# First layer's gate vectors: eight of 24 column blocks as whole dot products beside the last feature tiles' keys and values

## The chip, the cores and the metric

The kernel runs on one core of one Trainium2 chip. The metric is the device time of one execution in microseconds. TensorE (PE) multiplies, VectorE (DVE), ScalarE (ACT) and GpSimd (POOL) compute on tiles of 128 partitions, and SyncE (SP) issues all of this kernel's transfers, in order, from one queue. Each engine carries out its own instructions in order and waits where an operand or a buffer is not there yet.

## The reference

A trunk of two layers over 1024 latent tokens (`x`) and 256 context tokens (`ctx`), each 1024 wide. Cut to what matters here:

```python
silu_c, silu_cc = silu(c), silu(c_ctx)                  # two conditioning vectors of 1024
for i in range(2):
    shift, scale, gate = split(silu_c @ w_ada[i] + b_ada[i], 3)         # w_ada[i]: 1024 x 3072
    shift_c, scale_c, gate_c = split(silu_cc @ w_ada[i] + b_ada[i], 3)
    u  = h  * (1 + scale)   + shift
    uc = hc * (1 + scale_c) + shift_c
    y, yc = mixer(u, uc)          # layer 0: windowed attention, 4 key/value heads, rotary; layer 1: 2-D neighbourhood
    h  = layer_norm(sqrt(2) * h  + gate   * y)
    hc = layer_norm(sqrt(2) * hc + gate_c * yc)         # layer 0 only
```

The shift and scale of layer 0 are wanted first of all, since every feature of `u` hangs on them. The gate of layer 0 is wanted only after its attention, and with it the shift and scale of layer 1. These are 24 column blocks of 128 outputs, for two vectors each.

## The kernel before

All products are made in fp32 from a high and a low part of each operand (`hi`, `lo`, `wh`, `wl`, `uAh`, `uAl`): three matmuls stand for one.

**Start.** Features are taken in eight tiles (`kt`). For each, `mod_load` fetches the modulation weights (two tiles `wada` of 512 KB, from a ring of ten buffers) and the feature rows `hraw` (ring of four); `mod_rows` and `mod` make shift and scale on TensorE; `u_make` makes `uAh` and `uAl`; `k_mm` and `v_mm` add the tile's part to the keys (four PSUM banks `kp0_0`, `kp0_1`, `kp1_0`, `kp1_1`, and `kc`) and to the values of the first 512 tokens (`vps`). Value weights (`wv`) lie in buffers of the ring of ten too.

**After the last tile.** `rope_evac` turns the keys: VectorE shuffles a bank into `rb` and multiplies the bank by `cos` into `ra` (both read PSUM), GpSimd multiplies `rb` by `sin`, VectorE adds the two; `k_store` splits the sum into a tile `st` (ScalarE the high, VectorE the low part), which goes to memory (`kdA`). Meanwhile TensorE makes the values of the other tokens (`vproj_pieces`, banks `pv-1_2`, `pv-1_3`, `pv-1_4`) and the first query projection (`qprojA(0)`, banks `pj8_0` to `pj8_2`). The four banks of the keys are the only ones for these, so each waits for an eviction. The weights of a projection are split on the way: `wh` on ScalarE, `wl` on GpSimd; `wh8`/`wl8` hold features 0 to 511 and `wh9`/`wl9` the rest for `qprojA(0)`.

**Attention of layer 0.** Eight segments (`p`), each with 20 softmax blocks and, merged between them, the projections of the next heads. Beside them run the 24 column blocks, written as 48 half dots (`dot_half(h, j)`): a tile `gw` of 128 outputs by 512 inputs is loaded, VectorE reduces its product with `silu_c` (L617), GpSimd multiplies it by `silu_cc` (L618), and ScalarE sums that up (L599, issued with the next half dot by `dot_sum`). The numbers `SEG` say how many go into each segment; `dots_end` adds the halves and the bias.

What sets the order: the code is written in one sequence, and a list scheduler with priorities moves instructions on each engine, within the dependencies. The order on an engine is thus read from the built program, not from the code.

Of the kernel before, what the change touches and what calls it, by code (L numbers as in the profile page):

```python
# [11 lines left out]
F32 = mybir.dt.float32  # L12
F32R = mybir.dt.float32r
BF16 = mybir.dt.bfloat16
AF = mybir.ActivationFunctionType
ALU = mybir.AluOpType
# [3 lines left out]
P = 128  # L20
D = 1024
S = 1024
C = 256
T = S + C
# [13 lines left out]

GATED_LAST = 1 << 20

SEG = (7, 7, 7, 7, 7, 7, 6, 0)


def f32(ap):
# [38 lines left out]
def build(tc, i, out):  # L83
    nc = tc.nc
    mm = nc.tensor.matmul
    dma = nc.sync.dma_start
# [26 lines left out]
    dcol = cp.tile([P, 32, 2], F32, name="dcol")  # L113
# [4 lines left out]
    vdA = dr.tile([T, 4, P], F32, name="vdA")  # L118
# [140 lines left out]
    def v_evac(pl, vd):  # L259
        def evac(pt, b):  # L260
            st = st_tile(pl)
            for t in range(2):
                v = st[:, t].rearrange("p (h l d) -> p h l d", h=4, l=2)
                src = pt[:, t * 256 : (t + 1) * 256].rearrange("p (h d) -> p h d", h=4)
                nc.scalar.activation(v[:, :, 0, :], src, AF.Copy, scale=0.5)
                nc.vector.scalar_tensor_tensor(v[:, :, 1, :], src, 0.5, f32(v[:, :, 0, :]), ALU.mult, ALU.subtract)
            t0 = 2 * b * P
            dma(vd[t0 : t0 + 2 * P].rearrange("(t p) h e -> p t (h e)", p=P), f32(st))

        return evac  # L270
# [13 lines left out]
    def merge(att, fill, lead=0.0):  # L284

        ta = sum(a[0] for a in att) or 1.0
        tf = sum(f[0] for f in fill)
        ia = jf = 0
        ca = cf = 0.0
        while ia < len(att) or jf < len(fill):  # L290
            need = att[ia][2] if ia < len(att) and len(att[ia]) > 2 else 0
            if jf < len(fill) and (ia == len(att) or jf < need or cf - lead <= ca * (tf - lead) / ta):
                cf += fill[jf][0]
                fill[jf][1]()
                jf += 1
            else:
                ca += att[ia][0]
                att[ia][1]()
                ia += 1
# [162 lines left out]
    def rope_evac(store, pl, bufs):  # L462
        def evac(pt, t0, n):
            if t0 >= S:
                store(pt[:, :n], t0, n)
                return
            a = pl.tile([P, 512], F32, tag="ra", bufs=bufs, name="ra")
            b = pl.tile([P, 512], F32, tag="rb", bufs=bufs, name="rb")
            nc.vector.stream_shuffle(b, pt, SWAP)
            nc.vector.tensor_tensor(a, pt, cos[:, t0 : t0 + n], ALU.mult)  # L470
            nc.gpsimd.tensor_tensor(b, b, sin[:, t0 : t0 + n], ALU.mult)
            nc.vector.tensor_tensor(a, a, b, ALU.add)
            store(a, t0, n)

        return evac

    def k_store(nt):
        def store(src, t0, n):
            st = st_tile(pp)
            nc.scalar.copy(st[:, 0, :n], src)  # L480
            nc.vector.tensor_tensor(st[:, 1, :n], src, f32(st[:, 0, :n]), ALU.subtract)
            dma(kdA[:, nt * P : (nt + 1) * P, t0 : t0 + n].rearrange("l p t -> p l t"), f32(st[:, :, :n]))

        return store
# [67 lines left out]
    def v_mm(kt):  # L552
        hi, lo = w.got[VALUES[kt // 2]]
        sl = slice((kt % 2) * 256, (kt % 2 + 1) * 256)
        for t in range(4):
# [3 lines left out]
            mm(pt, lh, lo[:, sl], start=False, stop=False)  # L559
            mm(pt, ll, hi[:, sl], start=False, stop=kt == KT - 1 and t % 2 == 1)  # L560


    upto = (2, 3, 4, 4, 6, 7, 8, 8)
    for kt in range(-1, KT + 1):
        if kt + 1 < KT:
            for n in range(3) if kt < 0 else (kt + 3,) if kt + 3 < KT else ():
                mod_load(n, upto[n])
                if n == 0:
                    w.split(2)
            mod_rows(kt + 1)  # L570
        if kt > 0:
            k_mm(kt - 1)
        if kt + 1 < KT:
            mod(kt + 1)
        if kt < 0:

            warm(vps[:, 0:512], 12)
        if kt > 0:
            v_mm(kt - 1)
        if kt < KT and kt >= 0:  # L580
            u_make(kt)
            w.split(upto[min(kt + 1, 7)])
    dma(ident, i["ident"])
    dma(lnc, i["lnc"])
    dma(cos, i["cos"])
# [4 lines left out]


    dhalf = cp.tile([P, 24, 2], F32, name="dhalf")
    gh, sums = [], []

    def dot_sum():

        if sums:
            t, acc = sums.pop()
            tc.keep_in_program_order(nc.scalar.activation(t, t, AF.Copy, scale=0.5, accum_out=acc))  # L599

    def dot_half(h, j):
        def run():
            dot_sum()
            if j == 0:
                gh.clear()
                for v in range(2):
                    t = px.tile([P, 512], F32, tag=f"gh{v}", bufs=1, name="gh")
                    dma(t, bass.AP(i["cr"].tensor, v * D + h * 512, [[0, P], [1, 512]]))
                    th = px.tile([P, 512], F32, tag="gw", bufs=2, name="gth")
                    nc.scalar.activation(th, t, AF.Tanh, scale=0.5)  # L610
                    nc.vector.scalar_tensor_tensor(t, th, 1.0, t, ALU.add, ALU.mult)
                    gh.append(t)
            acc = dhalf if h else dcol
            t = px.tile([P, 512], F32, tag="gw", bufs=2, name="gw")
            dma(t, i["wadaT"][j, :, h * 512 : (h + 1) * 512])
            o = ap_.tile([P, 512], F32, tag="ra", bufs=1, name="gj")
            nc.vector.tensor_tensor_reduce(o, t, gh[0], 0.5, 0.0, ALU.mult, ALU.add, accum_out=acc[:, j, 0:1])  # L617
            nc.gpsimd.tensor_tensor(t, t, gh[1], ALU.mult)  # L618
            sums.append((t, acc[:, j, 1:2]))

        return (0.0, run, 0)

    def dots_end():
        dot_sum()
        for v in range(2):
            d = dcol[:, 0:24, v]
            nc.vector.tensor_tensor(d, d, dhalf[:, 0:24, v], ALU.add)
            nc.vector.tensor_tensor(d, d, bad[:, 16:40], ALU.add)
            shift, scale = dcol[:, 8:16, v], dcol[:, 16:24, v]
            nc.vector.scalar_tensor_tensor(colA[:, v, :], scale, 1.0, lnc[:, 0, :], ALU.add, ALU.mult)  # L630
            nc.vector.scalar_tensor_tensor(colB[:, v, :], scale, 1.0, lnc[:, 1, :], ALU.add, ALU.mult)
            nc.vector.tensor_tensor(colB[:, v, :], colB[:, v, :], shift, ALU.add)

    dots = [dot_half(h, j) for h in range(2) for j in range(24)]
    evs = []
    for c, (t0, n) in enumerate(CHUNKS):
        for nt in range(2):
            pt = kps[c, nt] if c < 2 else kc[:, nt * C : nt * C + C]
            evs.append((1.0, lambda nt=nt, pt=pt, t0=t0, n=n: rope_evac(k_store(nt), pp, 2)(pt, t0, n)))
    merge(evs, [])  # L640
    for b in range(2):
        v_evac(pp, vdA)(vps[:, b * 512 : (b + 1) * 512], b)
    merge([], vproj_pieces(-1, uA, v_evac(pp, vdA), 2))
    pp_st.close()
    pq, pq_st = pool("attA", "right")

# [692 lines left out]
```

## Time and profile before

| | us |
|---|---|
| median of three runs (lowest, highest) | 1449.84 (1449.49, 1455.52) |
| the profiled execution's own time | 1450.25 |
| its span | 1448.5 |
| TensorE busy in the span | 1393.6 (96%) |
| VectorE, ScalarE, GpSimd busy | 988.8, 733.9, 631.7 |
| granted TensorE clock, mean | 0.994 |

The time of an execution is 1.75 us longer than its span. A row of a timeline reads: start, duration, engine, line, operation, output<-inputs, shapes, count, and in brackets how long the engine stood idle before it and what ended that. A row of a group ends in: busy time, mean ns of one | idle time before, and what ended it. Engines in brackets after "waits" or "<-" are the ones that were waited for.

### The profile page before, as it was taken

The numbers are of one execution on the slowest core, as the hardware profiler recorded it, in microseconds if no ns is written. First come the engines' busy times: TensorE is split into PE (matmuls) and PEld (weight loads), VectorE is DVE, ScalarE is ACT, GpSimd is POOL, SyncE is SP. The second block draws the span as 40 slices with busy tenths as digits, with TensorE's granted clock in tenths as the row PEclk, the third lists the DMA queues.
The fourth block names the chain that finished last, engine by engine and source line by source line (L and its number), as shares of the span: only waits on it lengthen the run. The fifth ranks groups of instructions, "written<-read, shape, count | busy, mean of one in ns | idle before, by whom it ended". The sixth has DMA issues, their size and how long they took to land. (4 is left out here: it accounts for less than half of the span.)

```text
span 1448.5 us, 25148 instructions
## 1 busy us (share of the span) xinstructions
PE 1393.6 (96%) x8815; PEld 1217.2 (84%) x8816; DVE 988.8 (68%) x2216; ACT 733.9 (51%) x1561; POOL 631.7 (44%) x779
## 2 busy tenths in 40 slices
PE   8998999999999999999999999999999999998995
PEld 5887888888888888788888899888988898887775
DVE  4658887878888789566423766555565565667698
ACT  4336776677676778332222545554454444557310
POOL 0326666666666657233301333333233333336664
PEclk9999999999999999999999999999999999999998
DMA  9472114123222124434278565565555564384353
GB/s 369 172 227 85 60 48 131 45 77 101 68 70 62 56 67 131 133 129 136 75 216 230 156 195 152 150 166 146 168 147 152 146 182 140 102 207 151 114 133 93
DMA packets 117229, 195.05 MB, mean 135 GB/s; under 512 B 9328, under 2 KB 57840, under 8 KB 117104
## 3 DMA queue, kind: packets, MB, share of 16 engines
q1 hardware_dynamic: 117104, 193.45, 44.4%
q8 instruction: 70, 1.15, 0.3%
q14 instruction: 55, 0.45, 0.1%
HBM read 141.51 MB, written 51.90 MB: 134 GB/s over the span
## 5 line engine op out<-in xcount | busy, mean ns | idle before, releaser
L329 POOL TENSOR_SCALAR s_B<-s_B,rs_B 128x640 f32<-128x640 f32 (+1 forms) x128 | 101.1, 790 | 298.0 <-DVE rs_B L328 243.9
L208 PE MATMUL pj<-uBh,wh 128*128 128x512 f32 (+1 forms) x448 | 176.0, 393 | 0.0
L209 PE MATMUL pj<-uBl,wh 128*128 128x512 f32 (+1 forms) x448 | 170.3, 380 | 0.0
L210 PE MATMUL pj<-uBh,wl 128*128 128x512 f32 (+1 forms) x448 | 170.1, 380 | 0.0
L324 ACT ACTIVATE s_B<-s_B,m_B 128x640 f32<-128x640 f32 (+1 forms) x128 | 102.9, 804 | 131.2 <-DVE m_B L317 131.1
L324 ACT ACTIVATE s_A<-s_A,m_A 128x641 f32<-128x641 f32 (+2 forms) x160 | 119.5, 747 | 88.7 <-DVE m_A L317 73.7
L164 POOL TENSOR_TENSOR wl<-wr,wh 128x512 fp32r<-128x512 f32 x64 | 87.7, 1370 | 162.1 <-ACT wh L162 139.8
L329 POOL TENSOR_SCALAR s_A<-s_A,rs_A 128x640 f32<-128x640 f32 (+2 forms) x160 | 126.8, 793 | 58.0 <-DVE rs_A L328 55.7
L317 DVE CUSTOM_DVE_ANT_0 s_A<-S_A,msk,nsk 128x640 f32<-128x640 f32 (+2 forms) x160 | 123.6, 774 | 34.1 <-PE S_A L705 17.7
L342 DVE TENSOR_TENSOR pt_B<-T_B,pt_B 128x640 fp32r<-128x640 f32 (+1 forms) x128 | 100.9, 788 | 61.0 <-ACT pt_B L340 60.6
L208 PE MATMUL pj<-uAh,wh 128*128 128x512 f32 (+1 forms) x384 | 140.0, 365 | 0.0
L209 PE MATMUL pj<-uAl,wh 128*128 128x512 f32 (+1 forms) x384 | 137.8, 359 | 0.0
L210 PE MATMUL pj<-uAh,wl 128*128 128x512 f32 (+1 forms) x384 | 137.5, 358 | 0.0
L342 DVE TENSOR_TENSOR ptl_A<-T_A,pth_A 128x640 fp32r<-128x640 f32 (+2 forms) x160 | 114.0, 713 | 15.3 <-PE pvA L733 7.1
L336 PE MATMUL T_A<-ident,s_A 128*128 128x128 f32 x672 | 101.1, 275 | 12.2 <-DVE m_A L317 8.9
L336 PEld LDWEIGHTS T_A<-ident,s_A 128*128 128x128 f32 x672 | 77.2, 140 | 40.2 <-issue 16.7
L340 ACT CAST pt_B<-T_B 128x640 fp32r<-128x640 f32 (+1 forms) x128 | 84.3, 658 | 47.6 <-PE T_B L336 46.6
L317 DVE CUSTOM_DVE_ANT_0 s_B<-S_B,bias 128x640 f32<-128x640 f32 (+1 forms) x128 | 100.4, 784 | 10.5 <-PE S_B L1036 9.7
L340 ACT CAST pth_A<-T_A 128x640 fp32r<-128x640 f32 (+2 forms) x160 | 96.4, 603 | 16.8 <-PE T_A L336 14.1
L210 PEld LDWEIGHTS pj<-uBh,wl 128*128 128x128 f32 x448 | 84.3, 188 | 16.6
L336 PE MATMUL T_B<-ident,s_B 128*128 128x128 f32 x608 | 88.7, 275 | 9.9 <-DVE pt_B L342 5.0
L242 PE MATMUL pv<-wh,uBh 128*128 128x256 f32 x320 | 92.8, 291 | 3.1 <-ACT wh L162 3.1
(219 smaller groups left out, 3883.6 us busy)
## 6 DMA issues: line engine op xcount, KB each, us to landing
kB<-kdB SPq DMA_DIRECT2D x64, 320.0 KB, 5.2
gw<-in_wadaT SPq DMA_DIRECT2D x48, 256.0 KB, 2.8
vdB<-st SPq DMA_DIRECT2D x20, 512.0 KB, 3.2
vB<-vdB SPq DMA_DIRECT2D x16, 640.0 KB, 4.7
wada<-in_wadaC SPq DMA_DIRECT2D x16, 512.0 KB, 9.6
kdB<-st SPq DMA_DIRECT2D x16, 512.0 KB, 3.0
qdB<-st SPq DMA_DIRECT2D x16, 512.0 KB, 3.5
qB<-qdB SPq DMA_DIRECT2D x32, 256.0 KB, 4.7
```

What stands on the lines that cost most here:

```text
L164: e.tensor_tensor(lo, r, f32(hi), ALU.subtract)
L208: mm(pt[:, :n], hi[:, sl], rh, start=kt == 0, stop=False)
L209: mm(pt[:, :n], hi[:, sl], rl, start=False, stop=False)
L210: mm(pt[:, :n], lo[:, sl], rh, start=False, stop=kt == KT - 1)
L242: mm(pt, lh, hi[:, sl], start=kt == 0, stop=False)
L317: nc.vector.tensor_tensor_reduce(outp, sc, in1, scale, init if init is not None else 3e38, ALU.add, ALU.min, accum_out=s.m)
L324: nc.scalar.activation(s.t[:, :n], s.t[:, :n], AF.Exp, bias=s.m, scale=-1.0, accum_out=s.sum)
L329: nc.gpsimd.tensor_scalar(s.t[:, : s.w], s.t[:, : s.w], s.rs, 1.0, ALU.mult, ALU.mult)
L336: nc.tensor.transpose(tp[:, k * P : (k + 1) * P], s.t[:, src * P : (src + 1) * P], ident)
L340: nc.scalar.copy(pt.hi[:, :n, hl, :], tv)
L342: nc.vector.tensor_tensor(pt.lo[:, :n, hl, :], tv, f32(pt.hi[:, :n, hl, :]), ALU.subtract)
```

## The change

Column blocks 0 to 7 (the gate of layer 0; `PRE = 8`) leave attention and are made as whole dot products of 1024 inputs in the early stage. For that, the two vectors are loaded to all partitions (`silb`) and their silu (twice its value) is made there, once `mod_rows` of the later tiles has released buffers of the ring of ten; the weight tiles `gp0` to `gp7` come into the same ring. Each block is then one reduction on VectorE (`dcol[:, j, 0]`), one product in place on GpSimd, and one sum on ScalarE, as the half dots are, but twice as long. `early` puts the start of it beside tiles 5 to 7, and `pre_step` the rest between the evictions of the keys and the pieces of the values. The scratch output of the reduction takes a buffer of `hraw`. In attention 32 half dots (blocks 8 to 23) are left of 48, at most five a segment instead of seven.

```diff
--- before.py
+++ after.py
@@ -38,7 +38,8 @@
 
 GATED_LAST = 1 << 20
 
-SEG = (7, 7, 7, 7, 7, 7, 6, 0)
+PRE = 8
+SEG = (5, 5, 5, 5, 4, 4, 4, 0)
 
 
 def f32(ap):
@@ -559,6 +560,54 @@
             mm(pt, lh, lo[:, sl], start=False, stop=False)
             mm(pt, ll, hi[:, sl], start=False, stop=kt == KT - 1 and t % 2 == 1)
 
+    sums = []
+
+    def dot_sum():
+
+        if sums:
+            t, acc = sums.pop()
+            tc.keep_in_program_order(nc.scalar.activation(t, t, AF.Copy, scale=0.5, accum_out=acc))
+
+
+    dcol_pre, silb = {}, []
+
+    def pre_load(j):
+        dcol_pre[j] = pp.tile([P, D], F32, tag="wada", bufs=10, name=f"gp{j}")
+        dma(dcol_pre[j], i["wadaT"][j])
+
+    def pre_dot(j):
+        t = dcol_pre.pop(j)
+        o = pp.tile([P, T], F32, tag="hraw", bufs=4, name="junk")[:, :D]
+        nc.vector.tensor_tensor_reduce(o, t, silb[0], 0.5, 0.0, ALU.mult, ALU.add, accum_out=dcol[:, j, 0:1])
+        nc.gpsimd.tensor_tensor(t, t, silb[1], ALU.mult)
+        sums.append((t, dcol[:, j, 1:2]))
+
+    def early(kt):
+        if kt == 5:
+            for v in range(2):
+                t = pp.tile([P, D], F32, tag="wada", bufs=10, name=f"silb{v}")
+                dma(t, bass.AP(i["cr"].tensor, v * D, [[0, P], [1, D]]))
+                silb.append(t)
+        if kt == 6:
+            pre_load(0)
+            for t in silb:
+                th = pp.tile([P, T], F32, tag="hraw", bufs=4, name="th")[:, :D]
+                nc.scalar.activation(th, t, AF.Tanh, scale=0.5)
+                nc.vector.scalar_tensor_tensor(t, th, 1.0, t, ALU.add, ALU.mult)
+        if kt == 7:
+            pre_load(1)
+            pre_dot(0)
+        if kt == 8:
+            pre_step(2)
+
+    def pre_step(j):
+
+        dot_sum()
+        if j < PRE:
+            pre_load(j)
+        if j - 1 < PRE:
+            pre_dot(j - 1)
+
 
     upto = (2, 3, 4, 4, 6, 7, 8, 8)
     for kt in range(-1, KT + 1):
@@ -580,6 +629,7 @@
         if kt < KT and kt >= 0:
             u_make(kt)
             w.split(upto[min(kt + 1, 7)])
+        early(kt)
     dma(ident, i["ident"])
     dma(lnc, i["lnc"])
     dma(cos, i["cos"])
@@ -590,18 +640,12 @@
 
 
     dhalf = cp.tile([P, 24, 2], F32, name="dhalf")
-    gh, sums = [], []
-
-    def dot_sum():
-
-        if sums:
-            t, acc = sums.pop()
-            tc.keep_in_program_order(nc.scalar.activation(t, t, AF.Copy, scale=0.5, accum_out=acc))
+    gh = []
 
     def dot_half(h, j):
         def run():
             dot_sum()
-            if j == 0:
+            if j == PRE:
                 gh.clear()
                 for v in range(2):
                     t = px.tile([P, 512], F32, tag=f"gh{v}", bufs=1, name="gh")
@@ -623,24 +667,29 @@
     def dots_end():
         dot_sum()
         for v in range(2):
+            d = dcol[:, PRE:24, v]
+            nc.vector.tensor_tensor(d, d, dhalf[:, PRE:24, v], ALU.add)
             d = dcol[:, 0:24, v]
-            nc.vector.tensor_tensor(d, d, dhalf[:, 0:24, v], ALU.add)
             nc.vector.tensor_tensor(d, d, bad[:, 16:40], ALU.add)
             shift, scale = dcol[:, 8:16, v], dcol[:, 16:24, v]
             nc.vector.scalar_tensor_tensor(colA[:, v, :], scale, 1.0, lnc[:, 0, :], ALU.add, ALU.mult)
             nc.vector.scalar_tensor_tensor(colB[:, v, :], scale, 1.0, lnc[:, 1, :], ALU.add, ALU.mult)
             nc.vector.tensor_tensor(colB[:, v, :], colB[:, v, :], shift, ALU.add)
 
-    dots = [dot_half(h, j) for h in range(2) for j in range(24)]
+    dots = [dot_half(h, j) for h in range(2) for j in range(PRE, 24)]
     evs = []
     for c, (t0, n) in enumerate(CHUNKS):
         for nt in range(2):
             pt = kps[c, nt] if c < 2 else kc[:, nt * C : nt * C + C]
             evs.append((1.0, lambda nt=nt, pt=pt, t0=t0, n=n: rope_evac(k_store(nt), pp, 2)(pt, t0, n)))
+    evs = evs[:2] + [(1.0, lambda: pre_step(3))] + evs[2:4] + [(1.0, lambda: pre_step(4))] + evs[4:]
     merge(evs, [])
     for b in range(2):
         v_evac(pp, vdA)(vps[:, b * 512 : (b + 1) * 512], b)
-    merge([], vproj_pieces(-1, uA, v_evac(pp, vdA), 2))
+    pv = vproj_pieces(-1, uA, v_evac(pp, vdA), 2)
+    for n in range(PRE - 2):
+        pv.insert(1 + 5 * n, (0.0, lambda j=5 + n: pre_step(j)))
+    merge([], pv)
     pp_st.close()
     pq, pq_st = pool("attA", "right")
 
```

What the scheduler makes of it is seen at three places. On VectorE, after the last feature tile (`uAl` are its low parts; `kp0_0` is the first key bank; an ISA with `junk` is a reduction, the next one the read of its accumulator), the rows before are:

```order
L539 TENSOR_TENSOR uAl0_108<-hraw_472,uAh0_105 128x512
L539 TENSOR_TENSOR uAl2_110<-hraw_472,uAh2_107 128x256
L588 TENSOR_SCALAR nsk_142<-nsk_142 128x16
L469 STREAM_SHUFFLE rb_735<-kp0_0_144 128x512
L470 TENSOR_TENSOR ra_734<-kp0_0_144,cos_139 128x512
L469 STREAM_SHUFFLE rb_745<-kp0_1_145 128x512
L472 TENSOR_TENSOR ra_734<-ra_734,rb_735 128x512
L470 TENSOR_TENSOR ra_744<-kp0_1_145,cos_139 128x512
L469 STREAM_SHUFFLE rb_755<-kp1_0_146 128x512
```

and now:

```order
L596 SCALAR_TENSOR_TENSOR silb1_600<-th_666,silb1_600 128x1024
L581 ISA junk_710,dcol_71<-gp0_661,silb0_598 128x1024
L581 ISA dcol_71 128x1
L581 ISA junk_746,dcol_71<-gp1_708,silb0_598 128x1024
L581 ISA dcol_71 128x1
L470 STREAM_SHUFFLE rb_758<-kp0_0_144 128x512
L470 STREAM_SHUFFLE rb_768<-kp0_1_145 128x512
L581 ISA junk_780,dcol_71<-gp2_744,silb0_598 128x1024
L581 ISA dcol_71 128x1
L471 TENSOR_TENSOR ra_757<-kp0_0_144,cos_139 128x512
```

The second scaling of a silu row (the first stands ahead of `uAl0`) and three reductions, two ahead of the shuffles and one behind them, now come before the first product with `cos`, which is the last row. On GpSimd, in the same stretch (`rb` are the keys' sine products), before:

```order
L164 TENSOR_TENSOR wl8_946<-wr8_794,wh8_945 128x512
L471 TENSOR_TENSOR rb_735<-rb_735,sin_140 128x512
L164 TENSOR_TENSOR wl9_956<-wr9_796,wh9_955 128x512
L471 TENSOR_TENSOR rb_745<-rb_745,sin_140 128x512
L164 TENSOR_TENSOR wl10_986<-wr10_983,wh10_985 128x512
L471 TENSOR_TENSOR rb_755<-rb_755,sin_140 128x512
L164 TENSOR_TENSOR wl11_992<-wr11_989,wh11_991 128x512
L471 TENSOR_TENSOR rb_765<-rb_765,sin_140 128x512
L471 TENSOR_TENSOR rb_1025<-rb_1025,sin_140 128x512
```

and now:

```order
L582 TENSOR_TENSOR gp0_661<-gp0_661,silb1_600 128x1024
L582 TENSOR_TENSOR gp1_708<-gp1_708,silb1_600 128x1024
L582 TENSOR_TENSOR gp2_744<-gp2_744,silb1_600 128x1024
L472 TENSOR_TENSOR rb_758<-rb_758,sin_140 128x512
L472 TENSOR_TENSOR rb_768<-rb_768,sin_140 128x512
L472 TENSOR_TENSOR rb_784<-rb_784,sin_140 128x512
L472 TENSOR_TENSOR rb_794<-rb_794,sin_140 128x512
L165 TENSOR_TENSOR wl8_1004<-wr8_829,wh8_1003 128x512
L582 TENSOR_TENSOR gp3_778<-gp3_778,silb1_600 128x1024
L582 TENSOR_TENSOR gp4_804<-gp4_804,silb1_600 128x1024
L165 TENSOR_TENSOR wl9_1014<-wr9_831,wh9_1013 128x512
L582 TENSOR_TENSOR gp5_841<-gp5_841,silb1_600 128x1024
```

Before, GpSimd has the low parts `wl8` and `wl9` first and third in this stretch; now three products of 1024 and four sine products precede `wl8`, and two more products precede `wl9`. On VectorE, at the eviction of the values (`vps`) and of the first query bank `pj8_0`, before:

```order
L481 TENSOR_TENSOR st_774<-kc_148,st_774 128x256
L481 TENSOR_TENSOR st_778<-kc_148,st_778 128x256
L266 SCALAR_TENSOR_TENSOR st_782<-vps_149,st_782 128x4x64 x2
L266 SCALAR_TENSOR_TENSOR st_788<-vps_149,st_788 128x4x64 x2
L266 SCALAR_TENSOR_TENSOR st_847<-pv-1_2_798,st_847 128x4x64 x2
L266 SCALAR_TENSOR_TENSOR st_902<-pv-1_3_853,st_902 128x4x64 x2
L469 STREAM_SHUFFLE rb_1025<-pj8_0_999 128x512
```

and now:

```order
L581 ISA junk_910,dcol_71<-gp6_871,silb0_598 128x1024
L581 ISA dcol_71 128x1
L267 SCALAR_TENSOR_TENSOR st_817<-vps_149,st_817 128x4x64 x2
L581 ISA junk_938,dcol_71<-gp7_908,silb0_598 128x1024
L581 ISA dcol_71 128x1
L267 SCALAR_TENSOR_TENSOR st_823<-vps_149,st_823 128x4x64 x2
L470 STREAM_SHUFFLE rb_1083<-pj8_0_1057 128x512
L471 TENSOR_TENSOR ra_1082<-pj8_0_1057,cos_139 128x512
L267 SCALAR_TENSOR_TENSOR st_894<-pv-1_2_833,st_894 128x4x64
```

Reductions 6 and 7 stand between the value evictions, and `pj8_0` is read ahead of the banks `pv-1_2` and `pv-1_3` instead of behind them. With that goes another allocation of banks: `pj8_1` now takes the bank of `pj8_0`, where before it took that of `pv-1_2`. On SyncE's queue the loads of `silb`, `gp0`, `gp1` and `gp2` stand ahead of `ident`, `cos`, `sin` and the masks; `gp3` and `gp4` ahead of the first query weights; `gp5` to `gp7` between the stores of the keys; and `wr14` and `wr15`, which wait for GpSimd's `wl12` and `wl13`, ahead of the loads of `kA` instead of behind them.

## Prediction

> **What bounds the kernel now.** I read the page first, then the busy time by stretches, then TensorE's timeline through the first layer, and last VectorE and GpSimd where the change puts its work.
>
> ```profile
> span 1448.5 us, 25148 instructions
> PE 1393.6 (96%) x8815; PEld 1217.2 (84%) x8816; DVE 988.8 (68%) x2216; ACT 733.9 (51%) x1561; POOL 631.7 (44%) x779
> 58.00:98.00 40.00, 40.00 (x270) 37.11 (x269) 26.65 (x44) 11.77 (x25) 16.91 (x12) 1.00 0.58 186
> 98.00:165.00 67.00, 61.47 (x394) 53.42 (x393) 53.98 (x131) 44.74 (x103) 43.75 (x62) 1.00 0.35 100
> 165.00:527.00 362.00, 351.07 (x2285) 307.72 (x2283) 296.17 (x720) 251.64 (x573) 234.75 (x341) 1.00 0.23 73
> ```
>
> In the stretch rows the columns after the length are the busy time of TensorE (PE), its weight load, VectorE (DVE), ScalarE (ACT) and GpSimd (POOL). TensorE is the bound. Between 58 and 98 us (last feature tile, values, first projection) it has no gap at all, so any wait put there lengthens the run one for one. From 98 to 527 us, where the 48 half dots lie, it is idle for 5.53 + 10.93 = 16.5 us. That is all that the taking away of dots could ever give back; adding dots to the first stretch can only cost.
>
> How much of the 16.5 us belongs to dots shows in TensorE's and VectorE's rows beside them:
>
> ```profile
> 125.29 0.74 PE L336 MATMUL T_A<-ident,s_A 128*128 128x128 f32 x5 [1.30 <-POOL gw L618]
> 249.21 1.52 DVE L617 CUSTOM_DVE_ANT_0 gj<-gw,gh 128x512 f32<-128x512 f32 x1 [0.46 <-DMA gw<-in_wadaT]
> 251.70 0.74 PE L336 MATMUL T_A<-ident,s_A 128*128 128x128 f32 x5 [1.16 <-DVE m_A L317]
> 374.66 0.74 PE L336 MATMUL T_A<-ident,s_A 128*128 128x128 f32 x5 [1.16 <-DVE m_A L317]
> ```
>
> Three gaps have a dot directly ahead of them, 1.30 + 1.16 + 1.16 = 3.6 us; the rest repeats in every segment where the short context tiles are.
>
> **The change, part by part: what attention gets back.** Sixteen half dots leave the segments (48 become 32). Their busy time is no gain by itself, because TensorE covers it; the gain lies between 0 (the same gaps behind other dots) and the 3.6 us of the three gaps. With a third of the dots gone one gap of three would go by chance; wider spacing helps too. I take 2.0 us. One more gap could open behind a dot at a new place, up to 1.3 us as in the row at 125.29, so the lower end is -1.3. The final additions in dots_end keep their count.
>
> **What the early stage pays.** Eight whole dots are added, and two silu rows. The nearest prices:
>
> ```profile
> L617 DVE CUSTOM_DVE_ANT_0 gj<-gw,gh x48: 671/694/1523, 114.2 to 522.6; 128x512 f32<-128x512 f32 x48
> L618 POOL TENSOR_TENSOR gw<-gw,gh x48: 1262/1290/1306, 115.0 to 523.8; 128x512 f32<-128x512 f32 x48
> L909 DVE SCALAR_TENSOR_TENSOR z<-z,yA 128x1024 f32<-128x1024 f32 x9 | 10.9, 1210 | 0.0
> L1214 POOL TENSOR_TENSOR x<-x,vec 128x1024 f32<-128x1024 f32 x8 | 20.7, 2582 | 9.5 <-DMA x<-zdd 9.5
> L599 ACT ACTIVATE gw<-gw 128x512 f32<-128x512 f32 x48 | 30.2, 629 | 6.0 <-POOL gw L618 5.8
> L915 ACT ACTIVATE z<-z,rsd 128x1024 f32<-128x1024 f32 x10 | 12.4, 1243 | 34.3 <-issue 21.2 <-DVE rsd L914 13.1
> ```
>
> A whole dot is one reduction of 1024 on VectorE (1.25 us with its accumulator read), one product of 1024 on GpSimd (2.58 us) and one sum on ScalarE (1.24 us and a read of 0.19). Eight of them are 10.0 us of VectorE, 20.7 us of GpSimd and 11.4 us of ScalarE. By busy time all three fit into the 40 us stretch (26.65, 16.91 and 11.77 were used). They do not fit by order, for GpSimd and VectorE shut each other out:
>
> ```profile
> 61.95 1.28 POOL L164 TENSOR_TENSOR wl<-wr,wh 128x512 fp32r<-128x512 f32 x1
> 62.02 1.75 DVE L472 TENSOR_TENSOR ra<-ra,rb 128x512 f32<-128x512 f32 x1 [0.16 <-POOL rb L471]
> 63.19 1.76 POOL L471 TENSOR_TENSOR rb<-rb,sin 128x512 f32<-128x512 f32 x1
> 63.70 0.68 DVE L470 TENSOR_TENSOR ra<-kp,cos 128x512 f32<-128x512 f32 x1
> 72.68 0.69 DVE L472 TENSOR_TENSOR ra<-ra,rb 128x512 f32<-128x512 f32 x1
> ```
>
> L472 takes 0.69 us alone and 1.75 beside GpSimd's L164: it starts only when L164 is done, and GpSimd's L471 then waits for it. L470, which reads PSUM, runs beside GpSimd at 0.68. So where both operands are in SBUF the two engines take turns. Now the rows of the present stage that set the deadlines:
>
> ```profile
> 53.99 1.43 ACT L538 CAST uAh<-hraw 128x512 fp32r<-128x512 f32 x3
> 59.45 0.39 PE L550 MATMUL kp<-uAl,wh 128*128 128x512 f32 x1
> 63.88 0.28 PE L242 MATMUL pv-1_2_798<-wv,uAh 128*128 128x256 f32 x1
> 75.40 0.28 PE L242 MATMUL pv-1_4_908<-wv,uAh 128*128 128x256 f32 x1
> 81.16 0.39 PE L208 MATMUL pj<-uAh,wh 128*128 128x512 f32 x1
> 83.89 0.39 PE L208 MATMUL pj<-uAh,wh 128*128 128x512 f32 x1
> 86.61 0.39 PE L208 MATMUL pj<-uAh,wh 128*128 128x512 f32 x1
> 37.73 0.33 SPq L585 DMA_DIRECT2D cos<-in_cos  x1
> 50.39 1.08 PE L509 MATMUL kc<-wada,sil 128*32 128x128 f32 x32
> kA<-kdA SPq DMA_DIRECT2D x16, 320.0 KB, 5.0
> ```
>
> The silu rows: the two tanh (1.24 each) stand between the three casts of the last tile on ScalarE, the two scalings (1.2 each) between the three subtractions on VectorE. The last uAl ends near 58.0 instead of 56.2; TensorE asks for it at 59.45. Covered, cost 0; were silb late, this cover of 1.5 us would go. On SyncE's queue gp2 waits for the last modulation weights (51 us, the row at 50.39), and cos, sin and the masks stand behind it: issued near 52 instead of 37.7, landed near 57. VectorE asks for cos after 65. Cost 0.
>
> Then, instruction by instruction in the new order. (From here on, line numbers are those of the changed code, which are one higher in the evictions: its L471, L473 and L482 on VectorE are L470, L472 and L481 of the rows above.) The second scaling ends at 59.2, reduction 0 at 60.5, reduction 1 at 61.8; product 0 runs 61.8 to 64.4, and the two shuffles beside it; reduction 2 gets its turn at 64.4 to 65.7, and only then comes L471's reading of kp0_0 (66.4 us), on whose bank pv-1_2 waits: a stall of **2.5 us** against 63.88. Without the turn (reduction 2 at 63.2) it would be 1.2. GpSimd goes on with products 1 and 2 to 70.9 and the four sine products to 81.2, since each pair waits for VectorE to hand over a shuffled tile; kp1_0 is read at 78.6, against 75.40 + 2.5 for pv-1_4: **0.7 us**. Then turn by turn: reduction 3 (82.5), wl8 (83.7), L473 (84.3), product 3 (86.9), L482 and reduction 4 (88.8), L482 (89.4), product 4 (92.0), reduction 5 (93.3), wl9 (94.6). TensorE wants wl9 at the third matmul of the row at 83.89, 84.35 + 3.2 = 87.6: **7.0 us**. With no turns GpSimd would need 20.7 us of work and two hand-overs of some 1.5 us from 60.5 on, and wl9 would be there at 84.2: 0. I keep 7.0, since every pair in the rows above takes turns.
>
> No row shows a reduction (L617) holding GpSimd up: L618 never leaves 1262 to 1306 ns, for it always follows its own reduction. The Trainium skill (SBUF — State Buffer, "Who interferes with whom") says that an instruction of VectorE with two SBUF inputs contends with one of GpSimd that reads SBUF, and that whoever issues first has the port pair for its whole length. By that rule the reductions block GpSimd as L472 does, and the figure stays 7.0; were the reductions to block nothing, four times 1.25 us would leave the chain, and the stall would be 2.
>
> Next, pj8_1 takes the bank of pj8_0 (before, that of pv-1_2, long free), so it waits until VectorE has read pj8_0. That reading stands behind reductions 6 and 7, whose tiles are loaded behind the key stores on SyncE. At least shuffle and product (1.4 us) are waited for; with gp7 landing near 98 the reading is done at 102.4, while pj8_0 ends at 96.9: 5.5. The middle is **3.5**. After that pj8_2 and pj10_0 wait for value evictions behind ScalarE's sums (0 to 1.9), and the loads of kA stand behind vdA's stores and wr14/wr15, which wait for GpSimd's wl12 and wl13 (0 to 3.5, with 5.0 us to land). They hang on the longest chains, so I take half: **2.7**.
>
> Sum against the profiled execution (1450.25 us, 0.41 above the median of the three runs): 2.5 + 0.7 + 7.0 + 3.5 + 2.7 - 2.0 = +14.4, so **1464.6 us**. All terms at their low ends: 1.2 + 0 + 0 + 1.4 + 0 + 0 - 3.6 = -1.0, 1449; all at their high ends: 2.5 + 0.7 + 7.0 + 5.5 + 5.4 + 1.3 = +22.4, 1473.
>
> **The rivals.** (1) The stage absorbs most of it: reductions and products overlap better than the turns say, wl9 comes within 2 us of its need, and the bank wait stays near 2. Then 1.2 + 2 + 2 + 1 - 2 = +4, 1454, within 0.5% (7.2 us, about what a measurement here can tell from no change). For it speaks GpSimd's busy time, 16.9 of 40 us; against it that every contended pair is lengthened. (2) Faster: wl9 is there by 84.4 and kp0_0 is read by 63.9, no wait forms, and attention loses its three gaps: 1450.25 - 3.6 = 1446.6. It decides at GpSimd: three microseconds of slack in 23.9 (60.5 to 84.35). The one turn of reduction 1 ahead of product 0 takes 1.25 of them. Faster by over 0.5% needs twice the three gaps. (3) Worse: the kA loads' chain behind wr14 and wr15 grows past 3.5 us, and TensorE starves at the first transposes as well: 1475 and more. (4) The change not doing what it says is excluded by the order: the dots stand there.
>
> **How the numbers follow.** Forecast (waits of 9 to 22 us) 0.70; rival 1 0.20; rival 2 0.05, nearly all of it within 0.5%; rival 3 0.05. The range leaves out rival 2, the lower half of rival 1 and rival 3: 1454 to 1474; the likeliest case alone is 1457.5 to 1473. Slower by over 0.5% is the forecast and rival 3, with a little of the forecast falling short: 0.74; within 0.5% 0.23; faster 0.03.
>
> **What would show it.** In the profile after: between 58 and 125 us TensorE has gaps, ahead of pv-1_2 released by VectorE's L471, in pj8_0 by GpSimd's wl L165 (the largest), ahead of pj8_1 by VectorE; products L582 or reductions L581 have maxima near 2.5 to 3.8 us; the first S_A comes some 15 us later than 98.12. In attention the three gaps shrink to one or two. I am wrong if TensorE has no gap before 98 us (no turns at 1024), or if the attention segments shorten by more than 4 us in sum.

## The result and the profile after

| | before | after |
|---|---|---|
| median of four runs (lowest, highest), us | 1449.66 (1447.81, 1455.52) | 1465.07 (1464.44, 1468.71) |
| span of the profiled execution, us | 1448.5 | 1462.7 |

The ratio is 1.0116 (95% interval 1.0099 to 1.0133): the change costs 15.4 us where 14.4 were forecast. The page of the changed kernel, and its busy times in the stretches that the prediction showed (same columns):

```profile
span 1462.7 us, 25092 instructions
PE 1399.0 (96%) x8816; PEld 1220.5 (83%) x8816; DVE 993.4 (68%) x2202; ACT 736.2 (50%) x1547; POOL 629.0 (43%) x771
58.00:98.00 40.00, 31.20 (x210) 28.45 (x209) 35.29 (x44) 9.27 (x19) 29.46 (x14) 0.95 0.52 176
98.00:165.00 67.00, 56.65 (x307) 48.70 (x308) 41.22 (x93) 38.71 (x82) 33.38 (x43) 0.88 0.45 128
```

TensorE does the same matmuls (8816 records, 8815 before) but is busy 5.4 us longer, and its granted clock in the first two stretches is 0.95 and 0.88, where it was 1.00. To compare the same work, I cut each trace at the last matmul of vps (value blocks 0 and 1) and at the first and the last whole store of an attention segment to ogd. The columns are length, TensorE's busy time with its matmuls, granted clock, DMA share and GB/s. First before, then after:

```profile
63.75:178.91 115.16, 109.56 (x708) 1.00 0.41 125
178.91:544.06 365.15, 353.49 (x2304) 1.00 0.24 74
544.06:1448.50 904.44, 870.41 (x5277) 0.99 0.52 150
```

```profile
64.03:201.58 137.55, 117.51 (x708) 0.93 0.39 120
201.58:563.62 362.04, 353.20 (x2304) 1.00 0.21 65
563.62:1462.70 899.08, 867.82 (x5277) 0.99 0.52 151
```

The first stretch, from the end of the features to the end of the first attention segment, grows by 22.4 us: 14.4 us of idle time (5.60 to 20.04) and 8.0 us of busy time for the same 708 matmuls. The second, attention with 25 half dots instead of 38 (the other three that left stood in the first stretch), gives 3.1 us back. The third shrinks by 5.4 us though its work is the same; 2.7 us of that is one late weight load in the execution profiled before, which a second profile of the unchanged kernel does not have:

```profile
728.83 0.80 PE L242 MATMUL pv<-wh,uBh 128*128 128x256 f32 x2 [3.15 <-ACT wh L162]
```

```profile
726.78 0.50 PE L242 MATMUL pv<-wh,uBh 128*128 128x256 f32 x2 [0.47 <-ACT wh L162]
```

That third stretch took from 899.1 to 905.3 us in the profiles of this study, with no order in it that I found. A single profile's total is therefore good to some 3 us, and steps are better read from the stretch of 708 matmuls, which repeats to 0.1 us where there are two profiles of one kernel (115.16 and 115.22 before, 132.64 and 132.53 in experiment 10).

TensorE's gaps in the early stage of the changed kernel (idle time and what ended it in brackets):

```profile
65.46 0.38 PE L243 MATMUL pv-1_2_833<-wv,uAh 128*128 128x256 f32 x1 [1.15 <-DVE ra L471]
90.74 0.79 PE L211 MATMUL pj<-uAh,wl 128*128 128x512 f32 x1 [4.55 <-POOL wl L165]
100.12 0.80 PE L209 MATMUL pj<-uAh,wh 128*128 128x512 f32 x1 [5.21 <-DVE ra L471]
122.67 0.55 PE L753 MATMUL S_A<-kA,qA 128*128 128x256 f32 x1 [4.22 <-DMA kA<-kdA]
130.28 0.44 PE L753 MATMUL S_A<-kA,qA 128*128 128x384 f32 x1 [0.61 <-DVE m_A L318]
133.00 0.66 PE L337 MATMUL T_A<-ident,s_A 128*128 128x128 f32 x4 [1.86 <-POOL s_A L330]
135.43 1.09 PE L337 MATMUL T_A<-ident,s_A 128*128 128x128 f32 x4 [1.19 <-DVE m_A L318]
```

In order: value block 2 waits for a bank, pj8_0 for wl9, pj8_1 for the reading of pj8_0, the first S_A for its keys, and then the first score tiles starve. The first S_A stands at 122.67 instead of 98.12. The four waits ahead of it are 15.1 us of that. The order has a part too: 250 matmuls stand between the cut and the first S_A, 20 more than before. Most of the rest is slower matmuls, which the last section shows. VectorE and GpSimd just ahead of the second gap:

```profile
84.46 1.21 DVE L581 CUSTOM_DVE_ANT_0 junk<-gp,silb 128x1024 f32<-128x1024 f32 x1
86.20 3.36 DVE L581 CUSTOM_DVE_ANT_0 junk<-gp,silb 128x1024 f32<-128x1024 f32 x1
90.95 3.14 DVE L581 CUSTOM_DVE_ANT_0 junk<-gp,silb 128x1024 f32<-128x1024 f32 x1 [0.18 <-DMA gp<-in_wadaT]
```

```profile
85.76 2.72 POOL L582 TENSOR_TENSOR gp<-gp,silb 128x1024 f32<-128x1024 f32 x1 [1.77 <-DVE dcol L581]
88.44 2.24 POOL L165 TENSOR_TENSOR wl<-wr,wh 128x512 fp32r<-128x512 f32 x1
90.65 2.36 POOL L582 TENSOR_TENSOR gp<-gp,silb 128x1024 f32<-128x1024 f32 x1
```

A reduction takes 1.21 us alone. The one at 86.20 lasts until 89.56: it is shut out until the product ends at 88.48 and then runs its own 1.1 us, while the wl9 at 88.44 takes 2.24 us instead of 1.28. The turns that the prediction read from the keys' additions (L472) hold for the reductions too.

### The profile page after: what moved, and what is told of

It is laid out like the page before. It is cut to its first block, busy times and chain, and to the rows that moved or that the text cites. A ratio compares the mean times of both kernels' runs of the same rounds, so it can differ in the third digit from the quotient of the medians.

```text
span 1462.7 us, 25092 instructions
## 1 busy us (share of the span) xinstructions
PE 1399.0 (96%) x8816; PEld 1220.5 (83%) x8816; DVE 993.4 (68%) x2202; ACT 736.2 (50%) x1547; POOL 629.0 (43%) x771
## 3 DMA queue, kind: packets, MB, share of 16 engines
q8 instruction: 70, 1.15, 0.3%
## 5 line engine op out<-in xcount | busy, mean ns | idle before, releaser
L330 POOL TENSOR_SCALAR s_A<-s_A,rs_A 128x640 f32<-128x640 f32 (+2 forms) x160 | 122.7, 768 | 71.3 <-DVE rs_A L329 69.7
L753 PE MATMUL S_A<-kA,qA 128*128 128x384 f32 (+1 forms) x256 | 84.7, 354 | 9.2 <-DMA kA<-kdA 4.2
```

Source lines behind the costliest of these rows:

```text
L330: nc.gpsimd.tensor_scalar(s.t[:, : s.w], s.t[:, : s.w], s.rs, 1.0, ALU.mult, ALU.mult)
L753: mm(sc[:, 512 - n : 512], ql, kk[:, t0 : t0 + n], start=l == 0, stop=l == 1)
```

## The experiments

The first row in each fence is the stretch of 708 matmuls, in the columns above; below it stand the waits that decide. "Against before" is the median less that of the kernel before, run beside it on the same chip.

**1. The reductions short.**

```
- nc.vector.tensor_tensor_reduce(o, t, silb[0], ...)
+ nc.vector.tensor_tensor_reduce(o[:, :8], t[:, :8], silb[0][:, :8], ...)
```

> The changed kernel with the eight early reductions on VectorE cut from 1024 to 8 columns (the gate of layer 0 for the latent tokens is then not the right number); every engine's order of the waits in question stays. Theory (VectorE and GpSimd take turns where both read SBUF, and each turn lengthens GpSimd's chain): four to five turns of 1.2 us leave the chain ahead of wl9, its wait falls from 4.6 us to under 1, the wait for pj8_0's reading from 5.2 to about 2, and with shorter gaps the clock stays up: 1452 to 1457 us, that is 8 to 13 us less than the change. Rival 1 (GpSimd's own time for the products is enough): the wait for wl9 stays over 3 us, 1461 or more. Rival 2 (the transfers behind the gp loads on SyncE's queue set the waits): nothing moves, 1464.

1460.57 us, ratio 1.0093 (1.0076 to 1.0110), 13.1 against before.

```profile
64.05:193.03 128.98, 114.88 (x708) 0.93 0.42 128
95.08 0.79 PE L209 MATMUL pj<-uAh,wh 128*128 128x512 f32 x1 [7.79 <-DVE ra L471]
```

The wl9 wait is gone, as the theory has it, but most of the time is not: pj8_0 now ends 7.6 us earlier, its reading only 5.0 us earlier, and pj8_1's wait for it has grown from 5.21 to 7.79. The time went to the next wait in line: VectorE's reading now stands behind value evictions that wait for ScalarE.

**2. The products short.**

```
- nc.gpsimd.tensor_tensor(t, t, silb[1], ALU.mult)
+ nc.gpsimd.tensor_tensor(t[:, :8], t[:, :8], silb[1][:, :8], ALU.mult)
```

> The changed kernel with the eight early products on GpSimd cut from 1024 to 8 columns (the context tokens' gate is then not the right number). Theory and rival 1 both: 18.9 us leave GpSimd's queue, no turns are left, no wait for wl9 and none over 1.5 us for pj8_0's reading: 1444 to 1450 us. Rival 2 (SyncE's queue): the first S_A still waits 3 us or more for kA, and the time stays above 1454.

1455.79 us, ratio 1.0059 (1.0039 to 1.0078), 8.3 against before.

```profile
63.75:191.86 128.11, 115.98 (x708) 0.93 0.42 129
89.66 0.80 PE L209 MATMUL pj<-uAh,wh 128*128 128x512 f32 x1 [2.40 <-DVE ra L471]
112.01 0.55 PE L753 MATMUL S_A<-kA,qA 128*128 128x256 f32 x1 [4.61 <-DMA kA<-kdA]
```

No wait for wl9 and half the wait for pj8_0's reading, but the wait for the keys stays at 4.61. So rival 2's sign came, and its time: more than the engines' turns is at work.

**3. A second reduction on VectorE in place of GpSimd's product and ScalarE's sum.** It computes the same.

```
- nc.gpsimd.tensor_tensor(t, t, silb[1], ALU.mult)
- sums.append((t, dcol[:, j, 1:2]))
+ nc.vector.tensor_tensor_reduce(o, t, silb[1], 0.5, 0.0, ALU.mult, ALU.add, accum_out=dcol[:, j, 1:2])
```

> The changed kernel with the second vector's dot made as a second reduction on VectorE in place of GpSimd's product and ScalarE's sum; it computes the same. Theory: VectorE takes on 9.8 us more and stands at its limit of about 40 us between 58 and 100; four reductions stand ahead of the first key bank's reading (64 to 65.5 us against 63.9), the rest delays evictions by one to three microseconds each: total waits 2 to 6 us, 1449 to 1455 us. Rival 1 (GpSimd alone was the trouble): no waits, 1444 to 1447. Rival 2: the kA wait stays, 1456 or more.

1459.88 us, ratio 1.0090 (1.0075 to 1.0105), 12.4 against before.

```profile
64.22:191.58 127.36, 113.22 (x708) 0.95 0.41 126
96.28 0.80 PE L209 MATMUL pj<-uAh,wh 128*128 128x512 f32 x1 [8.05 <-DVE ra L471]
```

GpSimd is relieved, and VectorE, with sixteen reductions, is late: the wait moves to its reading of pj8_0. The theory has the direction right and its waits (2 to 6 us) too short, and the wait for kA, the sign of rival 2, is only 0.49 us.

**4. The kernel before without the sixteen half dots, and none put ahead** (the first eight gate columns then hold only their bias). What the change could have gained at best.

> The kernel before with the 16 half dots of blocks 0 to 7 left out and the same numbers per segment as the change has (the gate of layer 0 is then only its bias): the attention half of the change alone. Theory: the segments give 3 to 5 us back, and the 5 us that the changed kernel's profile shows to be gained after layer 0 come from a late weight load in the one profiled execution of before, not from the change: 1444 to 1447 us. Rival (the change shortens layer 1 too): 1440 to 1442. Rival (the dots cost attention nothing): 1449 to 1450.

1442.25 us, ratio 0.9965 (0.9952 to 0.9978), -5.3 against before.

```profile
64.08:175.12 111.04, 109.36 (x708) 1.00 0.40 123
```

TensorE's idle time in the stretch falls from 5.60 to 1.68, for the first segment's dots are in it (seven of them, ten before). The stretch is 4.1 us shorter and the second one 3.4 (361.74), more than the 3 to 5 us of the theory, and the median lies below its range.

**5. Reductions and products both short**, with loads, sums, order and banks as in the change.

> The change with its eight early reductions and its eight early products both cut to 8 columns; the loads, the sums on ScalarE, the order and the banks stay. Left out are therefore most of eight dot products. Theory (after the first call: the engines' turns are one part, and the order of the transfers and of the first S_A the other): no wait for wl9, pj8_1 still waits 1 to 3 us for the reading of pj8_0, the wait for kA of 4 to 5 us and the 3.7 us at the first transposes stay; 1453 to 1457. Rival (only the engines' work counts, and what e1 and e2 left is what each still had of it): none of these waits is longer than 1 us, and the time is 1443 to 1448, as with 16 half dots left out of attention and none put ahead.

1452.80 us, ratio 1.0030 (1.0020 to 1.0041), 3.8 against before.

```profile
63.95:187.71 123.76, 113.47 (x708) 0.96 0.41 128
108.68 0.55 PE L753 MATMUL S_A<-kA,qA 128*128 128x256 f32 x1 [3.47 <-DMA kA<-kdA]
ACT st L266 <- DMA kdA<-st: 4.9, 2, 3.2
```

With next to no work of the early dots left on VectorE and GpSimd, 8.6 us of the stretch remain against before. The theory's waits are there, with 1.88 us at pj8_1 and 3.7 at the first transposes; that for kA is shorter than it said, and the time just below its range. The last row (from ScalarE's waits between 58 and 118 us: total, times, longest) shows a value eviction held 3.2 us by a key store that had not landed: it needs that store's buffer, one of two.

**6. ScalarE's sums short as well**; only the eight loads of 512 KB keep their size. With the shorter sums the scheduler also puts the first S_A earlier: 244 matmuls behind the cut, not 250.

```
- sums.append((t, dcol[:, j, 1:2]))
+ sums.append((t[:, :8], dcol[:, j, 1:2]))
```

> The change with the reductions, the products and ScalarE's sums of the eight early dots all cut to 8 columns, and their loads of 128x1024 kept. Left out is most of eight dot products; ScalarE's sums are the one thing that differs from the run with both short at 1452.8, beside some rows near the first S_A that the scheduler puts otherwise. Theory (what is left there is the 4 MB of loads that share the DMA engines with the key stores, so that a store lands after 5.6 us instead of 1.5 us and its buffer holds the next eviction up): 1450 to 1453, and the wait of an eviction for a key store of about 3 us stays. Rival (it is the sums, 8 x 1.25 us of ScalarE between the casts and the evictions): 1443 to 1447, and no such wait.

1449.06 us, ratio 1.0001 (0.9986 to 1.0016), 1.0 against before.

```profile
67.11:185.66 118.55, 111.70 (x708) 0.99 0.43 133
93.05 0.75 PE L209 MATMUL pj<-uAh,wh 128*128 128x512 f32 x1 [2.92 <-DVE ra L471]
DVE junk L581 <- DMA gp<-in_wadaT: 3.0, 3, 2.1
```

The stretch is 5.2 us shorter (123.76 to 118.55), by the sums and by the earlier S_A together; this run does not part the two. The loads still make VectorE wait for gp, with pj8_0's reading queued behind, and a value eviction still waits up to 3.3 us for a key store. The cut stands 3 us later than elsewhere because the first modulation weights came late in this execution, a wait of 3.47 us at 13.19 us, long before the dots.

**7. The loads short as well**: instructions in the change's manner with next to no work in them.

```
- dma(dcol_pre[j], i["wadaT"][j])
+ dma(dcol_pre[j][:, :8], i["wadaT"][j, :, :8])
```

> As the kernel with the loads alone, but the eight loads too are cut to 8 columns: of the change stand the two silu rows, the instructions and their order, with next to no work in them. Theory (the engines' turns, the transfers and the sums make the whole loss, and the order costs little): 1441 to 1446, near the kernel before with 16 half dots left out (1442.25). Rival (the order and the banks that the scheduler takes are a loss by themselves): 1449 to 1454, with a wait of pj8_1 or for kA of 2 us or more still there.

1443.82 us, ratio 0.9969 (0.9956 to 0.9982), -4.3 against before.

```profile
63.96:175.77 111.81, 109.79 (x708) 1.00 0.41 124
91.59 2.57 SPq L727 DMA_DIRECT2D kA<-kdA  x4
```

Within 0.8 us of the stretch without these dots, and the kA loads are issued at 91.59 again (before at 91.70, in the change at 117.00). So this order costs next to nothing by itself. It is not quite the order of the change, though: the first S_A stands 232 matmuls behind the cut here, and 230 before. The starving at the first transposes goes by that place, whatever work the engines have: 3.7 us in all five profiles with 250 matmuls ahead (the change and experiments 1, 2, 3 and 5), 2.5 us, with the first pvA, in all three with 244 (experiments 6, 8 and 9), and no wait there over 0.4 us in this run. So that part goes with the order and is not lateness handed on, though no run moves the first S_A alone.

Experiments 4 to 7, 1, 2 and the change make a ladder on the same 708 matmuls:

| added to the rung above | stretch, us | idle, us | against before, median us |
|---|---|---|---|
| none of the early dots (4), S_A after 230 matmuls | 111.04 | 1.68 | -5.3 |
| the early instructions, 8 columns each (7), S_A after 232 | 111.81 | 2.02 | -4.3 |
| full loads (6), S_A after 244 | 118.55 | 6.85 | +1.0 |
| full sums on ScalarE (5), S_A after 250 as from here on | 123.76 | 10.29 | +3.8 |
| full reductions (2) | 128.11 | 12.13 | +8.3 |
| or full products (1) | 128.98 | 14.10 | +13.1 |
| both: the change | 137.55 | 20.04 | +15.4 |

The last four rows have one order. There reductions alone add 4.4 us, products alone 5.2, both 13.8, which is 4.2 more than the sum. That fits their turns on each other: the wait for wl9 (4.55 us) is there only with both.

**8. Half as many early dots** (PRE = 4, SEG = (6, 6, 6, 6, 6, 5, 5, 0)), computing the same.

> PRE = 4 and SEG = (6, 6, 6, 6, 6, 5, 5, 0): four whole dots ahead instead of eight, forty half dots in attention; it computes the same. The four reductions and products stand beside the last feature tiles and the key evictions; behind them no reduction stands ahead of pj8_0's reading, and two loads of wada less stand on SyncE between the value stores. Theory (the loss is in the late half: banks, late loads and the kA transfers behind them): no wait for wl9 or pj8_0's reading above 1 us, wait for kA under 2 us, 1445 to 1450. Rival (each dot costs its turns on the engines, some 2 us): half of the change's loss stays, 1453 to 1458.

1461.96 us, ratio 1.0093 (1.0073 to 1.0112), 12.9 against before.

```profile
64.37:192.46 128.09, 111.81 (x708) 0.96 0.36 111
98.91 0.76 PE L209 MATMUL pj<-uAh,wh 128*128 128x512 f32 x1 [10.10 <-DVE st L267]
98.33 0.42 DVE L267 SCALAR_TENSOR_TENSOR st<-pv-1_2_831,st 128x256 fp32r<-128x256 f32 x1 [0.45 <-ACT st L266]
```

There is no wait for wl9 and hardly one for kA (0.65 us), as the theory has it, but pj8_1 waits 10.10 us, and both expected times are wrong. The first four dots stand among the key evictions, whose sine multiplies are GpSimd's. The last key store is issued at 90.22 (90.90 in the change, 79.3 before), so all value evictions are late, and the scheduler gives pj8_1 the bank of value block 2, which is read only at 98.33. So four dots make the key stores as late as eight. The last four still add 9.5 us to the stretch (128.09 to 137.55, part of it by the later S_A), while attention, with 31 half dots in the second stretch instead of 25, takes 366.78 us there instead of 362.04. By the medians the last four are worth 2.5 us.

**9. Three buffers for st** instead of two, computing the same.

> The change with three buffers instead of two for st, the tile through which the key and value evictions go to DRAM; it computes the same. The scheduler's order then moves by some rows near the first S_A, and pj8_1 takes a bank other than that of pj8_0. Theory (the evictions wait for their stores, 8.1 us of ScalarE's waits between 58 and 118 us in the change, and through them value banks, kA loads and first S_A come late): the key stores end 3 to 4 us earlier, the wait of pj8_1 falls from 5.2 us below 2, the kA loads are issued 3 to 6 us earlier than at 117.00; 1455 to 1461. Rival (the backlog is GpSimd's, whose products keep the sine multiplies late, and the store waits lie beside it): first kdA store at 74 as before, the wait for wl9 stays at 4 to 5 us, and the time is 1461 to 1467.

1461.00 us, ratio 1.0080 (1.0062 to 1.0098), 12.9 against before.

```profile
63.98:192.33 128.35, 114.58 (x708) 0.96 0.42 129
98.95 0.77 PE L209 MATMUL pj<-uAh,wh 128*128 128x512 f32 x1 [4.32 <-DVE st L267]
110.89 2.45 SPq L727 DMA_DIRECT2D kA<-kdA  x4
```

Half right: kA is loaded 6.1 us earlier, its wait down to 0.25, while the first key store stays at 74.2, wl9 is still waited for (2.92 us) and pj8_1 still waits 4.32, now for a value bank. The buffers were a link of the chain, not its start.

**10. Idle matmuls in two gaps**, run twice.

```
+ if (j0, ci, kq) == (8, 0, 4):
+     idle(u, 11)      # into an unused PSUM tile
  mm(pt[:, :n], lo[:, sl], rh, start=False, stop=kt == KT - 1)
  ...
+ if (j0, ci) == (8, 0): idle(u, 13)
```

> The change, with 11 matmuls of 128x512 into an unused PSUM tile placed ahead of the matmul that waits 4.55 us for wl9, and 13 behind the last matmul of pj8_0, ahead of the pj8_1 that waits 5.21 us (0.39 us each, so 4.3 and 5.1 us). VectorE, GpSimd and the transfers keep their work; the scheduler also moves the first S_A up by some 30 rows in TensorE's order, so the verdict is read from the rows between 84 and 110 us. Theory (the gaps lower TensorE's granted clock, and the same matmuls then take longer): with the gaps filled the clock stays at 1.00 between 87 and 107 us, where the change shows 0.50 to 0.80 in windows of 3 us, and the matmuls from the wl9 wait to the end of pj8_2 end 3 to 6 us earlier; 1456 to 1462 in all. Rival (the lower clock comes from something else, such as the power of the other engines, or costs nothing because the engine waits anyway): the clock is as low as before in those windows, and the time 1464 to 1468.

> The kernel with the two gaps filled by idle matmuls, once more, in five rounds, since its trace was 5.5 us ahead of the change at the first store of attention and its median only 1.4 us. Theory (a gap costs more than its length, because TensorE's clock is lower behind it): ratio to the kernel before 1.006 to 1.009 and the stretch from 58 us to the first store of attention 138 us again instead of 143.6. Rival (the 5.5 us are given back later, or were that one execution's): ratio 1.010 to 1.013.

1463.66 us, ratio 1.0103 (1.0086 to 1.0119), and 1465.29 us, ratio 1.0111 (1.0092 to 1.0129). The second run's rows:

```profile
63.88:196.41 132.53, 120.62 (x732) 0.96 0.40 125
90.80 5.03 PE L194 MATMUL idle<-uAh 128*128 128x512 f32 x11 [4.76 <-DVE st L491]
98.90 3.20 PE L194 MATMUL idle<-uAh 128*128 128x512 f32 x13 [0.30 <-DVE st L276]
99.00:102.00 3.00, 3.00 (x13) 1.00 0.00 0
102.00:105.00 3.00, 2.97 (x14) 1.00 0.80 261
```

The first filling failed: its tile took a buffer that VectorE was still reading, so the eleven stand behind the gap and only delay pj8_0 by 4.8 us. The second worked, and there the clock is 1.00 in both windows where the change has 0.50 and 0.59. The stretch is 4.9 and 5.0 us shorter, part of which is the first S_A's earlier place (232 matmuls behind the cut): the starving at the first transposes is gone. The medians cannot be told from the change's, and the second ratio is the one that the rival named. So the clock's recovery is shown in the rows, and its price in the total stays open.

## Why the prediction was right, term by term

The mechanism and the places of the waits were right. That the size came out right is in part luck: some 12 us of cost were not in the sum (the clock and the first transposes), the gain was sized too small, and the two errors offset each other.

- **wl9, 7.0 forecast, 4.55 measured.** It was to be the largest wait and came second, for the chain of turns ended earlier: wl9 was ready at 90.68 instead of 94.6. The turns are shown by the rows at 86.20 and 88.44, and experiments 1 and 2 take the wait away from either side. The Trainium skill (SBUF — State Buffer, "Who interferes with whom") says that two SBUF inputs on VectorE contend with GpSimd's reads and that the first to issue keeps the ports; the rows agree, with 3.36 us for a reduction of 1.21.
- **pj8_1, 3.5 forecast (1.4 to 5.5), 5.21 measured**, in the range, and half for the reason given. pj8_0's reading stands behind the last two reductions, but these were late by turns with the products (3.14 and 2.39 us where one alone takes 1.21), not by their loads: gp was waited for 0.18 us, and the last reduction began at 95.22, where the forecast had gp7 landing near 98.
- **Keys and value evictions, 2.7 forecast (0 to 5.4), 4.22 measured**, all of it at kA, whose loads stand behind wr14 and wr15 as forecast; pj8_2 and pj10_0 did not wait. **pv-1_2, 2.5 forecast, 1.15 measured; pv-1_4, 0.7 forecast, 0 measured.** Together 16.4 against 15.1.
- **Rival 3's starving at the first transposes came too**: 0.61 + 1.86 + 1.19 = 3.7 us, by the first S_A's later place (experiment 7), while the small gaps that before has at its own start of attention, part of its 5.60 us of idle time, are gone.
- **Left out of the sum: TensorE's clock, 8.0 us of busy time in the profiled execution.** The forecast priced a wait at its length ("one for one"). The mean granted clock of whole executions was 0.985 to 0.990 in the four runs of the change and 0.992 to 0.997 in those of before.
- **Attention's gain was sized too small.** Forecast 2.0, at most 3.6; experiment 4 measures 5.3 us by medians and 4.1 + 3.4 us in the two stretches of its profile. That is more than the 4 us that the prediction named as a sign of being wrong, so this term failed by its own test. The early stage then costs 15.4 + 5.3 = 20.7 us by medians, not 16.4; the ratios 1.0116 and 0.9965 lie 0.0151 apart, 22 us. The profiles of the change and of experiment 4 differ by 26.5 us in the first stretch, which the waits (15.1), the first transposes (3.7) and the clock (8.0) nearly make up. Why the medians show less is open.
- **Loads and sums were costed as order only.** The prediction let them lie beside other work, apart from what the queue does. The ladder gives 6.7 us of the stretch to the loads and 5.2 to the sums, each with the later place of the first S_A that came with it; up to 3.7 us of the two together, and slower matmuls behind, are that place's. The cover was there by busy time, not at the places where evictions, stores and loads follow one another.
- Rival 1, that the stage absorbs most, holds only where the engines' work is taken out (experiments 5 and 6). None of the variants that compute the same beats the kernel before.

## What to carry to other kernels

A gap in TensorE may cost more than its length: in these profiles every gap of 2.40 us or more came with a granted clock of 0.50 for 3.4 us or longer, though what that adds to a whole execution is not shown. When work is added beside a chain of evictions, stores and loads through few buffers, ask what stands at the head of that chain, because later waits can be the same lateness handed on, and taking one away shows the next. A ladder that puts the work back one engine at a time on the same matmuls separates them better than totals do, as long as the order on the bounding engine stays the same from rung to rung.

## What the hardware showed that I had not expected

The clock falls at a gap and comes back after some microseconds. In the changed kernel, first by windows of 3 us and then the four pieces of the early stage in which the granted clock was 0.50 (the columns as above):

```profile
99.00:102.00 3.00, 1.88 (x5) 0.50 0.00 0
102.00:105.00 3.00, 3.00 (x10) 0.59 0.84 253
105.00:108.00 3.00, 3.00 (x16) 1.00 0.76 267
90.78:94.20 3.42, 3.42 (x8) 0.50 0.96 253
97.61:104.44 6.83, 4.32 (x10) 0.50 0.29 81
121.50:128.33 6.83, 5.66 (x15) 0.50 1.09 273
135.16:138.57 3.41, 3.14 (x14) 0.50 0.95 297
```

The four pieces go with the gaps at wl9, pj8_1, kA and the first transposes. Some begin while the gap still lasts, and each is 3.4 or 6.8 us long. TensorE is busy for 16.5 of their 20.5 us; at half the clock that is 8.3 us of extra time, which accounts for the 8.0 us. The gap of 2.40 us in experiment 2 does it too: matmuls of 512 columns then start 0.43 us apart for 3 us, 0.23 later.

Length alone does not decide it. In the 14 profiles every gap of 2.40 us or more comes with such a piece. Of the shorter ones some do, such as 1.85 us (experiment 9, at 738.14) and 2.11 us (before, at 1332.72), and others do not, such as 1.88 us (pj8_1 in experiment 5) and 2.35 us (experiment 9, at 1343.69). The 1.86 and 1.19 us at the first transposes, which follow each other within 3 us, do; the single gap of 1.15 us (pv-1_2 here) does not. The Trainium skill (TensorE: Matmul & The Clock Gate, "HAM oscillation — how this bites in real kernels") warns of idle gaps over about 3.4 us. The gaps over 4 us agree; that of 2.40 us shows a drop below that length.
